# Sparse attention of a two-layer decoder: query norm applied before the split, compressed softmax in two steps

## The chip, the cores and the metric

The kernel runs on one core of one Trainium2 chip. The metric is the time of one execution on the device in microseconds (us), measured beside other runs of the same kernel; the median of three runs of the kernel before is 995.87 us (995.0 to 997.96). Engines are named as in the profile: PE is TensorE, DVE is VectorE, ACT is ScalarE, POOL is GpSimd, SP is SyncE.

## The reference, cut to what matters

The whole program is a decoder trunk of two layers on 256 tokens of width 1024. Each layer has two SwiGLU half-steps around an attention: stick-breaking in the first layer, a sparse attention with three branches in the second. The change lies in the second attention alone:

```python
proj = hn @ w_in
q = proj[..., :NSA_HEADS * Dh].reshape(B, S, NSA_HEADS, Dh)
q = _apply_rope(_rmsnorm(q, q_norm), cos, sin).reshape(B, S, G, R, Dh)
gates = jax.nn.sigmoid(proj[..., NSA_HEADS * Dh:]...)
s_c = jnp.einsum('btgrd,bcgd->bgrtc', q, k_c) * scale
p_c = jax.nn.softmax(jnp.where(valid_c, s_c, NEG), axis=-1) * any_valid
o_c = jnp.einsum('bgrtc,bcgd->btgrd', p_c, v_c)
...
o_s = _nsa_selected(q, sel_idx, k_s, v_s)
o_w = _nsa_window(q, k_w, v_w)
o = gates[0] * o_c + gates[1] * o_s + gates[2] * o_w
return o.reshape(B, S, NSA_HEADS * Dh) @ w_out
```

There are 16 query heads of 64 columns in 4 groups that share keys and values. The root-mean-square norm of a query is one number per token and head. Rotation (rope) and the scores are linear in the query, so that number can be multiplied in anywhere between the projection and the exponential.

## The kernel before, in words

Tokens lie in two tiles of 128 partitions. All arithmetic is to single precision: each operand of a matmul is split into a part that TensorE takes exactly (`hi`, a rounded copy made on ScalarE) and a remainder (`lo`, a subtraction on VectorE), and `mm3` (lines 289 to 292) issues three matmuls for each product. Weights go through the same split: `Weights.pump` (line 201) copies on ScalarE (line 222) and subtracts on VectorE (line 226).

The program is written as one list. A list scheduler orders each engine's instructions by their place in the text and by when their inputs are expected, so that an instruction that is expected late lets others pass; `tc.keep_in_program_order` holds one at its place. On the chip each engine takes its list strictly in order.

The sparse attention is the function `nsa` (line 1332). Its queries come in three projection blocks of two, three and three pairs of heads (`Q_BLOCKS`), each computed in four pieces (`proj_block`, line 587). For a block:

- `q_evac` (line 1348) takes the projection out of PSUM with the weights of the norm (line 1356, VectorE) and its squares (line 1359, ScalarE); block 0 also has the gates.
- `q_turn` (line 1371) rotates on GpSimd (lines 1375 to 1379), splits (ScalarE copy, line 1380; VectorE subtraction, line 1381) and then works out the norm factor `rq`: a sum on VectorE (line 1385), logarithm and exponential on ScalarE (1387, 1388), and four tiny GpSimd operations, one Newton step (1389 to 1392). The factor isn't multiplied into the queries.
- `q_trans` (line 1394) transposes the split queries on TensorE, into banks `aux` (two, taken in turn), and copies them to `qs` (line 1404, ScalarE).

For each of the 16 heads then:

- `scores` (line 1406) issues eight matmuls (line 1417) for masks and scores of both token tiles against own, window and compressed keys; VectorE takes the negated maxima of four pieces (1434, 1435) and multiplies them by the norm factor (1437); ScalarE makes four exponentials with bias and scale from memory (1440 of 128 columns, 1445 of 256), each followed by a read of its accumulated sum, and copies the compressed scores to `cs` (1442); VectorE inverts the sums (1449), GpSimd multiplies in the gate (1450) and scales the probabilities `P` (1453, 256 and 512 columns).
- `ptrans` (line 1480) transposes the probabilities, three transposes for each of two branches (line 1492), and splits them (ScalarE 1494, VectorE 1495); the tiles are named `PT` or, where an old tile is used again, `hT_m`.
- `values` (line 1497) issues six matmuls against the values into `O`; each fourth call adds the compressed branch and splits the output (1515, 1516).

The compressed scores of four heads together go through `cmp_soft` (line 1455): maximum (VectorE 1459), subtraction (GpSimd 1460), product with the norm factor (GpSimd 1461), exponential (ScalarE 1463), sum and inverse (VectorE 1464, 1465), and two GpSimd products with the gate (1466, 1469). `cmp_trans` (line 1471) transposes and splits the result.

The order is written out by hand. While blocks 1 and 2 are projected, the table `plan` (line 1523) says what follows piece i of block b: the transposes of block 0's queries after piece (1, 2), scores of heads 0, 1 and 2 after (1, 3), (2, 0) and (2, 1), the transposes of block 1 and of head 0's probabilities after (2, 2). Then come scores 3, `ptrans(1)`, scores 4, and the loop at line 1560 over n from 1 to 15: a weight split, at n = 1 the whole `q_turn` of block 2, its transposes at n = 3 and n = 6, `cmp_soft` at n = 1, 4, 8 and 12, `cmp_trans` at n = 3, 7, 11 and 15, `ptrans(n + 1)`, `scores(n + 4)`, from n = 12 on a part of the output projection, and `values(n - 1)`.

Of the kernel before, what the change touches and what calls it, by code (L numbers as in the profile page):

```python
# [258 lines left out]
def build(tc, ctx, a, out):  # L259
# [1072 lines left out]
    def nsa(hT, rs, post, targets, st):  # L1332
        kD, V, vcB = st["kD"], st["V"], st["vcB"]
        tc.keep_in_program_order(nc.scalar.preload_act_table_set("natural_log_exp_and_others"))
        with tc.tile_pool(name="ns", bufs=1) as sp:
# [9 lines left out]
            qw, Pm, PT, cs, Ox = {}, {}, {}, {}, {}  # L1345
            heads = [(2 * sc + i, hh) for sc in range(4) for hh in range(2) for i in range(2)]

            def q_evac(b, o):
# [20 lines left out]
                return lambda: q_turn(w, sq, n, h0)  # L1369

            def q_turn(w, sq, n, h0):
                hi, qv = w[:, :, 0:n, 0, :], w[:, :, 0:n, 1, :]
                c, sn = [cst[:, x:x + 32].rearrange("p (t i) -> p t i", t=2).unsqueeze(2) for x in (C_COS, C_SIN)]
# [5 lines left out]
                nc.gpsimd.tensor_tensor(qv[:, :, :, 0:16], t1, t2, op=OP.add)  # L1379
                nc.scalar.activation(hi.bitcast(R), qv, AF.Copy)  # L1380
                nc.vector.tensor_tensor(qv, qv, hi, op=OP.subtract)
                r = rq[:, :, h0:h0 + n]
# [23 lines left out]
            def scores(n, banks=accs):  # L1406
# [26 lines left out]
                r = rq[:, :, 2 * p + hh]  # L1433
# [3 lines left out]
                nc.vector.tensor_tensor(m, m, r.unsqueeze(2).to_broadcast([P, 2, 2]), op=OP.mult)  # L1437
                pr = Pm[n] = sp.tile([P, 768], F32, tag="P", bufs=4, name="P")
                for b in range(2):
                    nc.scalar.activation(pr[:, b * P:(b + 1) * P], va[:, b, :], AF.Exp, bias=nm[:, 0, b:b + 1],  # L1440
                                         scale=r[:, 0:1], accum_out=nm[:, 1, b:b + 1])
                nc.scalar.activation(cs[sc][:, :, 2 * (p % 2) + hh, :], sa[:, 256:288].rearrange("p (t c) -> p t c", t=2),
                                     AF.Copy)
                for b in range(2):
                    nc.scalar.activation(pr[:, 256 + b * 256:512 + b * 256].rearrange("p (k s) -> p k s", k=2),
                                         vb[:, b, :, :], AF.Exp, bias=nm[:, 0, 2 + b:3 + b],
                                         scale=r[:, 1:2], accum_out=nm[:, 1, 2 + b:3 + b])
# [6 lines left out]

            def cmp_soft(sc):

                v = cs[sc].rearrange("p t n i -> p (t n) i")
                mx = sp.tile([P, 2, 8], F32, tag="cm", bufs=2, name="cm")
                nc.vector.tensor_reduce(mx[:, 0, :], v, axis=AX.X, op=OP.max)
                nc.gpsimd.tensor_tensor(v, v, mx[:, 0, :].unsqueeze(2).to_broadcast([P, 8, 16]), op=OP.subtract)  # L1460
                nc.gpsimd.tensor_tensor(cs[sc], cs[sc], rq[:, :, 4 * sc:4 * sc + 4].unsqueeze(3).to_broadcast([P, 2, 4, 16]),
                                        op=OP.mult)
                nc.scalar.activation(v, v, AF.Exp)
                nc.vector.tensor_reduce(mx[:, 0, :], v, axis=AX.X, op=OP.add)
# [53 lines left out]
            def zbanks(name):  # L1518
# [4 lines left out]
            plan = {(1, 2): [lambda: q_trans(0)],  # L1523
                    (1, 3): [lambda: scores(0, zbanks)],
                    (2, 0): [lambda: scores(1)],
                    (2, 1): [lambda: scores(2, zbanks)],
                    (2, 2): [lambda: q_trans(1), lambda: ptrans(0)]}
            for b in range(3):
                o = accs("qp")
                n = Q_COLS[b]  # L1530
                pc = proj_block(n, hT, b == 0, post, [x[:, 0:n] for x in o])
                for i, f in enumerate(pc):
                    f()
                    for g in plan.get((b, i), ()):
                        g()
                turn = q_evac(b, o)
                if b < 2 or not True:
                    turn()
# [21 lines left out]
            for n in range(1, 16):  # L1560
# [4 lines left out]
                if n == 1:  # L1565
                    turn()
                if n == 3:
# [3 lines left out]
                if n == 1 or n % 4 == 0:  # L1571
                    cmp_soft(sc)
# [4 lines left out]
                if n + 4 < 16:  # L1577
                    scores(n + 4)
                if n >= 12:
# [189 lines left out]
```

## Time and profile before

| | us |
|---|---|
| median of 3 runs | 995.87 |
| lowest, highest | 995.0, 997.96 |
| the profiled execution | 994.79 |
| its span (first to last instruction) | 993.0 |

| engine | busy us, whole span | instructions |
|---|---|---|
| PE | 983.4 | 4961 |
| DVE | 873.7 | 1149 |
| ACT | 698.2 | 1099 |
| POOL | 114.9 | 184 |

The sparse attention, from its first projection to its output projection, lies at about 714 to 810 us of the span; its loop over the heads begins at about 745. In rows in order of time, the columns are start, duration, engine, line, operation, output and input, shape and count; the bracket at the end of a row is the idle time of the engine ahead of it and what ended it. In rows of groups, the mean duration in ns stands after the busy time. Instructions of one engine overlap at their ends, so that the distance between two starts can be shorter than the duration of the first.

### The profile page before, as it was taken

To read this page: it belongs to the slowest core of one execution; us is meant where nothing else is said; L and a number is where in the kernel's file an instruction comes from. 1 tells how busy PE (TensorE), PEld (TensorE's weight loads), DVE (VectorE), ACT (ScalarE), POOL (GpSimd) and SP (SyncE) were. 2 spreads that over 40 slices of the span, in tenths; PEclk is the share of its full clock that TensorE was granted. 3 is DMA by queue.
4 is the path that set the end of the run, shared out by engine and by line. 5 is a ranking of instruction groups with operands and counts; after the bars stand their busy time and mean duration, and the time that the engine had idled before them with its cause. 6 is when DMAs were issued, how large, how long until landed. Compare 5 with 4: busy or idle time off the path is not lost.

```text
span 993.0 us, 14093 instructions
## 1 busy us (share of the span) xinstructions
PE 983.4 (99%) x4961; PEld 817.1 (82%) x4961; DVE 873.7 (88%) x1149; ACT 698.2 (70%) x1099; POOL 114.9 (12%) x184
## 2 busy tenths in 40 slices
PE   9999999999999999999999999999999999999998
PEld 6787888898988788878888887888897888788887
DVE  7899999878879999999778698898668879999996
ACT  6776767577868767777565775666669958767763
POOL 0000000010000000000217101000056500000000
PEclk9999999999999999999999999999999999999999
DMA  9988774599846978775996789667330186977761
GB/s 332 355 244 254 222 211 144 176 303 292 247 151 225 332 230 250 235 208 171 273 318 206 252 278 245 235 207 219 114 121 1 45 311 228 310 231 216 250 170 43
DMA packets 65479, 219.89 MB, mean 221 GB/s; under 512 B 7168, under 2 KB 9216, under 8 KB 65408
## 3 DMA queue, kind: packets, MB, share of 16 engines
q1 hardware_dynamic: 58336, 197.86, 58.3%
q0 software_dynamic: 6784, 20.97, 12.1%
q8 instruction: 39, 0.64, 0.3%
q14 instruction: 32, 0.26, 0.1%
q10 hardware_dynamic: 288, 0.16, 0.1%
HBM read 212.67 MB, written 13.63 MB: 228 GB/s over the span
## 4 chain that ended last, share of the span: by engine, by line
PE 69%; issue 13%; DVE 8%; DMA 4%; ACT 3%; POOL 2%; SPq 0%; ACTq 0%; DVEq 0%; POOLq 0%
PE o L291 6%; PE o L292 6%; PE o L290 6%; PE c L290 5%; PE c L292 5%; PE c L291 5%; DVE wl L226 4%; PE a L290 3%; PE a L292 2%; PE a L291 2%; PE cu L290 2%; PE cu L292 2%; PE cu L291 2%; DMA keep<-in_f1i 2%; PE qk L948 2%
## 5 line engine op out<-in xcount | busy, mean ns | idle before, releaser
L226 DVE TENSOR_TENSOR wl<-wraw,wh 128x1024 fp32r<-128x1024 f32 (+2 forms) x316 | 377.1, 1210 | 37.4 <-ACT wh L222 35.7
L222 ACT ACTIVATE wh<-wraw 128x1024 fp32r<-128x1024 f32 (+2 forms) x316 | 322.6, 1044 | 71.1 <-PE o L292 23.8
L222 ACT ACTIVATE wh<-keep 128x1024 fp32r<-128x1024 f32 x112 | 116.6, 1056 | 68.5 <-DVE keep L234 48.8
L226 DVE TENSOR_TENSOR wl<-keep,wh 128x1024 fp32r<-128x1024 f32 x112 | 132.7, 1216 | 6.2 <-ACT wh L222 5.9
L234 DVE TENSOR_TENSOR keep<-keep,wraw 128x1024 f32<-128x1024 f32 x80 | 97.2, 1215 | 1.6 <-DMA wraw<-in_f1i 1.6
L291 PE MATMUL o<-wl,gTh0f 128*128 128x512 f32 x192 | 75.0, 391 | 0.3 <-DVE wl L226 0.3
L290 PE MATMUL o<-wh,gTh0f 128*128 128x512 f32 x192 | 74.8, 397 | 0.0
L292 PE MATMUL o<-wh,gTl0f 128*128 128x512 f32 x192 | 74.6, 391 | 0.0
L290 PE MATMUL o<-wh,gTh1f 128*128 128x512 f32 (+1 forms) x160 | 62.5, 399 | 0.0
L291 PE MATMUL o<-wl,gTh1f 128*128 128x512 f32 (+1 forms) x160 | 62.1, 388 | 0.0
L292 PE MATMUL o<-wh,gTl1f 128*128 128x512 f32 (+1 forms) x160 | 61.3, 388 | 0.0
L290 PE MATMUL a<-wh,hT_f 128*128 128x512 f32 x144 | 57.5, 399 | 0.0
L290 PE MATMUL c<-wh,hT_f 128*128 128x512 f32 x144 | 56.6, 393 | 0.0
L292 PE MATMUL a<-wh,hT_f 128*128 128x512 f32 x144 | 56.3, 391 | 0.0
L291 PE MATMUL a<-wl,hT_f 128*128 128x512 f32 x144 | 56.3, 391 | 0.0
L291 PE MATMUL c<-wl,hT_f 128*128 128x512 f32 x144 | 56.2, 390 | 0.0
L292 PE MATMUL c<-wh,hT_f 128*128 128x512 f32 x144 | 56.2, 390 | 0.0
L290 PE MATMUL cu<-wh,sums 128*128 128x512 f32 x112 | 44.6, 398 | 1.0 <-ACT cp L754 1.0
L290 PE MATMUL c<-wh,sums 128*128 128x512 f32 x112 | 44.3, 396 | 0.1
L292 PE MATMUL cu<-wh,sums 128*128 128x512 f32 x112 | 43.8, 391 | 0.0
L292 PE MATMUL c<-wh,sums 128*128 128x512 f32 x112 | 43.7, 390 | 0.0
L291 PE MATMUL c<-wl,sums 128*128 128x512 f32 x112 | 43.6, 389 | 0.0
(346 smaller groups left out, 2365.0 us busy)
## 6 DMA issues: line engine op xcount, KB each, us to landing
wraw<-in_f1i SPq DMA_DIRECT2D x76, 512.0 KB, 4.8
wraw<-in_f2i SPq DMA_DIRECT2D x68, 512.0 KB, 5.0
wraw<-in_f1o SPq DMA_DIRECT2D x44, 512.0 KB, 4.7
wraw<-in_f2o SPq DMA_DIRECT2D x44, 512.0 KB, 4.8
wraw<-in_sbqk SPq DMA_DIRECT2D x16, 512.0 KB, 4.6
wraw<-sf SPq DMA_DIRECT2D x16, 512.0 KB, 4.5
keep<-in_f2i SPq DMA_DIRECT2D x16, 512.0 KB, 4.5
keep<-in_f2i POOLq DMA_DIRECT2D x16, 512.0 KB, 8.8
```

Source lines behind the costliest of these rows:

```text
L222: i = nc.scalar.activation(hi[:, 0:n], raw[:, 0:n], AF.Copy)
L226: e.tensor_tensor(lo[:, 0:n], raw[:, 0:n], hi[:, 0:n].bitcast(F32), op=OP.subtract)
L234: nc.vector.tensor_tensor(t, y, raw, op=OP.add)
L290: nc.tensor.matmul(o, xh, wh, start=start, stop=False, skip_group_check=True)
L291: nc.tensor.matmul(o, xh, wl, start=False, stop=False, skip_group_check=True)
L292: nc.tensor.matmul(o, xl, wh, start=False, stop=stop, skip_group_check=True)
L948: nc.tensor.matmul(oi, wh[:, c], xh, start=k == 0 and q == 0, stop=False, skip_group_check=True)
```

## The change

Queries are multiplied by their norm factor on GpSimd between rotation and split (`q_scale`). So scores come out normed: the product of the maxima with the factor, the scale operands of the four exponentials, and the product of the compressed scores with the factor go. `q_turn` becomes four steps, rope, norm, scale and split. Blocks 0 and 1 run all four at once; block 2 runs them at n = 1 (rope ahead of the transposes, norm after the scores), n = 2 and n = 3, and its first transposes move from n = 3 to n = 4. The compressed softmax is cut in two: maximum and subtraction (`cmp_max`) at n = 1, 4, 8 and 12, now after the scores, and the rest (`cmp_soft`) at n = 2, 5, 9 and 13, with its exponential and sum held in program order. Everything in `plan` moves one piece later.

```diff
-                return lambda: q_turn(w, sq, n, h0)
+                return q_turn(w, sq, n, h0)
 
             def q_turn(w, sq, n, h0):
                 hi, qv = w[:, :, 0:n, 0, :], w[:, :, 0:n, 1, :]
+                return [lambda: q_rope(qv, n), lambda: q_norm(sq, n, h0), lambda: q_scale(qv, n, h0), lambda: q_split(hi, qv)]
...
+            def q_scale(qv, n, h0):
+                nc.gpsimd.tensor_tensor(qv, qv, rq[:, :, h0:h0 + n].unsqueeze(3).to_broadcast([P, 2, n, DH]), op=OP.mult)
+
+            def q_split(hi, qv):
                 nc.scalar.activation(hi.bitcast(R), qv, AF.Copy)
                 nc.vector.tensor_tensor(qv, qv, hi, op=OP.subtract)
...
-                m = nm[:, 0, :].rearrange("p (t b) -> p t b", t=2)
-                nc.vector.tensor_tensor(m, m, r.unsqueeze(2).to_broadcast([P, 2, 2]), op=OP.mult)
...
                     nc.scalar.activation(pr[:, b * P:(b + 1) * P], va[:, b, :], AF.Exp, bias=nm[:, 0, b:b + 1],
-                                         scale=r[:, 0:1], accum_out=nm[:, 1, b:b + 1])
+                                         accum_out=nm[:, 1, b:b + 1])
...
-                                         scale=r[:, 1:2], accum_out=nm[:, 1, 2 + b:3 + b])
+                                         accum_out=nm[:, 1, 2 + b:3 + b])
...
-            def cmp_soft(sc):
+            def cmp_max(sc):
...
                 nc.gpsimd.tensor_tensor(v, v, mx[:, 0, :].unsqueeze(2).to_broadcast([P, 8, 16]), op=OP.subtract)
-                nc.gpsimd.tensor_tensor(cs[sc], cs[sc], rq[:, :, 4 * sc:4 * sc + 4].unsqueeze(3).to_broadcast([P, 2, 4, 16]),
-                                        op=OP.mult)
-                nc.scalar.activation(v, v, AF.Exp)
-                nc.vector.tensor_reduce(mx[:, 0, :], v, axis=AX.X, op=OP.add)
+
+            def cmp_soft(sc):
...
+                tc.keep_in_program_order(nc.scalar.activation(v, v, AF.Exp))
+                tc.keep_in_program_order(nc.vector.tensor_reduce(mx[:, 0, :], v, axis=AX.X, op=OP.add))
...
-            plan = {(1, 2): [lambda: q_trans(0)],
-                    (1, 3): [lambda: scores(0, zbanks)],
-                    (2, 0): [lambda: scores(1)],
-                    (2, 1): [lambda: scores(2, zbanks)],
-                    (2, 2): [lambda: q_trans(1), lambda: ptrans(0)]}
+            plan = {(1, 3): [lambda: q_trans(0)],
+                    (2, 0): [lambda: scores(0, zbanks)],
+                    (2, 1): [lambda: scores(1)],
+                    (2, 2): [lambda: scores(2, zbanks)],
+                    (2, 3): [lambda: q_trans(1), lambda: ptrans(0)]}
...
                 if n == 1:
-                    turn()
-                if n == 3:
+                    rope()
+                if n == 4:
                     q_trans(2, (5,))
...
-                if n == 1 or n % 4 == 0:
-                    cmp_soft(sc)
...
+                if n == 1:
+                    norm()
+                if n == 2:
+                    scale()
+                if n == 3:
+                    split()
+                if n == 1 or n % 4 == 0:
+                    cmp_max(sc)
+                if n == 2 or n % 4 == 1 and n > 1:
+                    cmp_soft(sc)
```

More of the change, by code (lines that the diff above doesn't have):

```diff
@@ L1344, in nsa @@
                 nc.gpsimd.memset(x[64:128].bitcast(F32), 0.0)
-            qw, Pm, PT, cs, Ox = {}, {}, {}, {}, {}
+            qw, Pm, PT, cs, cm, Ox = {}, {}, {}, {}, {}, {}
             heads = [(2 * sc + i, hh) for sc in range(4) for hh in range(2) for i in range(2)]
@@ L1379, in q_turn, with q_norm @@
                 nc.gpsimd.tensor_tensor(qv[:, :, :, 0:16], t1, t2, op=OP.add)
+            def q_scale(qv, n, h0):
+                nc.gpsimd.tensor_tensor(qv, qv, rq[:, :, h0:h0 + n].unsqueeze(3).to_broadcast([P, 2, n, DH]), op=OP.mult)
+            def q_split(hi, qv):
                 nc.scalar.activation(hi.bitcast(R), qv, AF.Copy)
                 nc.vector.tensor_tensor(qv, qv, hi, op=OP.subtract)
+            def q_norm(sq, n, h0):
                 r = rq[:, :, h0:h0 + n]
@@ L1453, in scores @@
                     nc.gpsimd.tensor_tensor(x, x, nm[:, 2, j:j + 2].unsqueeze(2).to_broadcast([P, 2, w]), op=OP.mult)
+            def cmp_max(sc):
+                v = cs[sc].rearrange("p t n i -> p (t n) i")
+                mx = cm[sc] = sp.tile([P, 2, 8], F32, tag="cm", bufs=2, name="cm")
+                nc.vector.tensor_reduce(mx[:, 0, :], v, axis=AX.X, op=OP.max)
+                nc.gpsimd.tensor_tensor(v, v, mx[:, 0, :].unsqueeze(2).to_broadcast([P, 8, 16]), op=OP.subtract)
             def cmp_soft(sc):
                 v = cs[sc].rearrange("p t n i -> p (t n) i")
[L1458 to L1461, printed above, removed]
-                                        op=OP.mult)
-                nc.scalar.activation(v, v, AF.Exp)
-                nc.vector.tensor_reduce(mx[:, 0, :], v, axis=AX.X, op=OP.add)
+                mx = cm[sc]
+                tc.keep_in_program_order(nc.scalar.activation(v, v, AF.Exp))
+                tc.keep_in_program_order(nc.vector.tensor_reduce(mx[:, 0, :], v, axis=AX.X, op=OP.add))
                 nc.vector.reciprocal(mx[:, 0, :], mx[:, 0, :])
@@ L1536, in nsa @@
                 turn = q_evac(b, o)
-                if b < 2 or not True:
-                    turn()
+                while b < 2 and turn:
+                    turn.pop(0)()
+            rope, norm, scale, split = turn
             oo = None
@@ L1565, in nsa @@
                 if n == 1:
-                    turn()
-                if n == 3:
+                    rope()
+                if n == 4:
                     q_trans(2, (5,))
```

2 lines of the change are left out of this document (1 added, 1 removed).

## The prediction

> **What bounds the kernel now.** I read the page's span and busy rows first, then the busy time by stage over the sparse attention, then ScalarE's and TensorE's rows in order of time there, and last the groups of that stretch.
>
> ```profile
> span 993.0 us, 14093 instructions
> PE 983.4 (99%) x4961; PEld 817.1 (82%) x4961; DVE 873.7 (88%) x1149; ACT 698.2 (70%) x1099; POOL 114.9 (12%) x184
> ```
>
> Over the whole program TensorE is the engine that is never free, and 70% for ScalarE (ACT) looks harmless. The stages say otherwise. The columns are span, then busy time and count for PE, PEld, DVE, ACT and POOL, then the granted clock, the DMA share and GB/s:
>
> ```profile
> 715.00:727.24 12.24, 12.24 (x78) 11.85 (x77) 10.87 (x19) 8.49 (x16) 4.54 (x8) 1.00 0.73 232
> 727.24:744.77 17.53, 17.44 (x114) 15.44 (x114) 10.48 (x25) 12.41 (x40) 9.81 (x21) 1.00 0.16 58
> 744.77:787.24 42.47, 40.30 (x271) 33.70 (x270) 34.44 (x90) 41.25 (x155) 26.48 (x52) 1.00 0.01 1
> 787.24:798.00 10.76, 10.76 (x58) 8.84 (x57) 10.14 (x17) 9.90 (x16) 4.15 (x7) 1.00 0.53 179
> ```
>
> From 744.77 to 787.24, the loop over the heads, ScalarE works 41.25 of 42.47 us; nowhere else in the attention is it that full. PE shows 40.30, but its matmul ends are modelled, so I price its work by starts. One head's three parts follow, each met once with nothing waiting: the scores from 763.37 to 764.49, the values from 764.49 to 765.62 with the eight query transposes behind them to 766.49, six probability transposes from 772.08 to 772.73. The first and the last row bound the eleven heads that I count.
>
> ```profile
> 743.52 0.29 PE L1417 MATMUL S<-mns,identb 128*128 128x288 bf16 x1
> 763.37 0.30 PE L1417 MATMUL S<-mns,identb 128*128 128x288 bf16 x1
> 764.49 0.48 PE L290 MATMUL O<-PT,Vh 128*128 128x512 f32 x1
> 765.62 1.04 PE L1402 MATMUL qTp<-cst,qw 128*128 128x128 f32 x8
> 766.49 0.29 PE L1417 MATMUL S<-mns,identb 128*128 128x288 bf16 x1
> 772.08 0.82 PE L1492 MATMUL pt<-cst,P 128*128 128x128 f32 x6
> 772.73 0.27 PE L1417 MATMUL S<-mns,identb 128*128 128x256 bf16 x1
> 781.01 0.30 PE L1417 MATMUL S<-mns,identb 128*128 128x288 bf16 x1
> ```
>
> So a score group is 1.12 us of PE, a head's values 1.13, its transposes 0.65. Between 743.52 and 781.01 stand eleven score groups (12.3), ten heads' values (11.3) and transposes (6.5), twelve query transposes at 0.87 for eight (1.3), and about 1.8 for the twelve compressed-value matmuls and four small transposes (an estimate: half a values matmul each): 33.2 of 37.49 us. PE therefore has 4.3 us of stops in the loop. That is the most the loop can give before PE itself is the limit, however fast the others get. These rows are where the stops are plainest; the bracket names the wait and what ended it, and in the second row three transposes take 0.88 instead of half of 0.82:
>
> ```profile
> 746.63 0.28 PE L1417 MATMUL S<-mns,identb 128*128 128x288 bf16 x1 [0.34 <-ACT cs L1442]
> 749.66 0.88 PE L1492 MATMUL pt<-cst,P 128*128 128x128 f32 x3
> 752.14 0.50 PE L290 MATMUL O<-hT_m,Vh 128*128 128x512 f32 x1 [0.90 <-ACT hT_m L1494]
> 768.75 0.49 PE L290 MATMUL O<-hT_m,Vh 128*128 128x512 f32 x1 [0.25 <-ACT hT_m L1494]
> 769.62 0.38 PE L1475 MATMUL ct<-cst,cs 128*64 128x128 f32 x2 [0.38 <-DVE hT_m L1495]
> ```
>
> Three of the four named waits end with ScalarE, the fourth with a VectorE copy that stands behind ScalarE's. ScalarE paces the loop, TensorE is close behind.
>
> **The exponentials lose their scale operand.** Each of the 16 heads has four, with a bias and a scale read from memory per partition. In the loop ScalarE's starts follow each other without gaps, so the step from one start to the next is its price:
>
> ```profile
> 744.77 0.84 ACT L1380 ACTIVATE qw<-qw 128x768 fp32r<-128x768 f32 x1 [0.50 <-POOL qw L1379]
> 745.52 0.44 ACT L1440 ACTIVATE P<-S,nm,rq 128x128 f32<-128x128 f32 x1
> 745.86 0.19 ACT L1440 ACTIVATION_READ_ACCUMULATOR P<-S,nm,rq 128x1 f32 x1
> ...
> 746.47 0.57 ACT L1445 ACTIVATE P<-S,nm,rq 128x256 f32<-128x256 f32 x1
> 746.92 0.21 ACT L1445 ACTIVATION_READ_ACCUMULATOR P<-S,nm,rq 128x1 f32 x1
> ...
> 750.92 0.31 ACT L1463 ACTIVATE cs<-cs 128x128 f32<-128x128 f32 x1 [0.70 <-POOL cs L1461]
> ...
> 751.24 0.85 ACT L1494 ACTIVATE hT_m<-pt 128x384 fp32r<-128x384 f32 x2
> 751.98 0.46 ACT L1440 ACTIVATE P<-S,nm,rq 128x128 f32<-128x128 f32 x1
> ```
>
> An exponential of 128 columns steps 0.34, one of 256 steps 0.45; one of 384 would step 0.56. A plain copy of 384, without operands, steps 0.37 (two in 0.74). Two operands are thus worth 0.19, one 0.09. The one-operand copy against the plain one says the same, 475 against 379 ns:
>
> ```profile
> L1135 ACT ACTIVATE kva<-kv,rstd 128x256 f32<-128x256 f32 x4 | 1.9, 475 | 3.6 <-PE kv L292 3.6
> L620 ACT ACTIVATE rBqk<-rB 128x256 f32<-128x256 f32 x1 | 0.4, 379 | 0.0
> L1445 ACT ACTIVATE P<-S,nm,rq 128x256 f32<-128x256 f32 x26 | 15.0, 609 | 0.0
> L1453 POOL TENSOR_TENSOR P<-P,nm 128x512 f32<-128x512 f32 x12 | 12.5, 1043 | 0.0
> L1453 POOL TENSOR_TENSOR P<-P,nm 128x256 f32<-128x256 f32 x12 | 7.4, 615 | 0.9
> L1437 DVE TENSOR_TENSOR nm<-nm,rq 128x4 f32<-128x4 f32 x12 | 2.5, 204 | 0.2
> L1461 POOL TENSOR_TENSOR cs<-cs,rq 128x128 f32<-128x128 f32 x3 | 1.2, 404 | 0.2
> ```
>
> No exponential with a bias alone is in this trace: the saving lies between 0 (both reads overlap) and 0.19, and I take 0.09, the one-operand row. The loop has 26 pairs (x26 at L1445 and as many at L1440), so 52 x 0.09 = 4.7 us of ScalarE's 42.47 go; the other twelve exponentials lie beside the projection and pay nothing.
>
> **What else leaves the loop.** The product of maximum and norm (L1437, 204 ns a head on VectorE) goes, ahead of the exponentials. On POOL the product of compressed scores and norm goes (404 ns). ScalarE stood 0.70 us at 750.92 behind that, inside the third block's norm; with the maximum taken one head and the exponential the next, POOL has a head's time, and I take that wait as gone. The third block's split, 0.75 of step at 744.77 ahead of the first head's exponentials, moves to n = 3. It is still paid, where ScalarE then has room.
>
> **What is added.** Three products on POOL, in place. L1453 gives 1.04 us for 512 columns and 0.62 for 256, so 1.04 for the first block and, by the same slope, 1.47 for the others. In the loop that is 1.47 less three times 0.40, on an engine busy 26.48 of 42.47: nothing on the path, since the third block's queries are needed at n = 4 and the product is issued at n = 2. If POOL's cover went, it would cost its 1.47. The matmuls stay as they are.
>
> **What is moved.** Query transposes and the first three score groups come one projection piece later. PE's work is the same, but behind the last piece nothing of the projection is left to fill waits: query transposes of block 1, head 0's transposes, scores 3, head 1's transposes, scores 4. ScalarE must empty the two banks these transposes alternate in, which before had projection matmuls beside it. And block 0 has a longer way to its transposes: norm, product, split. Before:
>
> ```profile
> 724.07 1.86 POOL L1389 TENSOR_TENSOR qn<-qn 128x8 f32<-128x8 f32 x1 [2.55 <-ACT qn L1388]
> ...
> 726.59 0.20 POOL L1392 TENSOR_TENSOR rq<-qn 128x8 f32<-128x8 f32 x1
> 723.18 2.69 DVE L226 TENSOR_TENSOR wl<-wraw,wh 128x768 fp32r<-128x768 f32 x3
> 722.22 0.69 DVE L1381 TENSOR_TENSOR qw<-qw 128x512 f32<-128x512 f32 x1 [0.46 <-ACT qw L1380]
> 721.55 0.63 ACT L1380 ACTIVATE qw<-qw 128x512 fp32r<-128x512 f32 x1 [1.49 <-POOL qw L1379]
> 727.24 0.30 PE L1417 MATMUL S<-mns,identb 128*128 128x288 bf16 x1
> ```
>
> PE reached head 0's scores at 727.24, right behind piece four of block 1; without the 0.87 of query transposes ahead it gets there at 726.4 and now wants the transposes. If the norm is ready at 726.8 as before, product (1.04), split (0.63) and subtraction (0.69) end at 729.2, 2.8 us late. The norm no longer waits for the subtraction of 722.22, though, and three short POOL products need not take until 726.8; and projection matmuls can go first where the list order lets them. Between 0 and 2.8 us I take 0.5, near the lower end, because PE still has block 2's projection to put ahead.
>
> **The sum.** Of 4.3 us of PE stops I keep 1.2: waits for the compressed transposes, the third block's split (0.75) in its new place, and the limit that PE and ScalarE, now at 36.5 (42.47 less 4.7 and its 1.22 idle) against 38.2, share (38.2 is 42.47 less 4.3). The loop gives 3.1; the start costs 0.5. The profiled execution took 994.79 us (span 993.0 and 1.8 around it), so 994.79 - 2.6 = 992.2; the median of the three runs, 995.87, is 1.08 above that execution, and I forecast 993.3. Behind 787.24 PE is busy 10.76 of 10.76, so nothing more is won there and, as the weight loads follow the loop, nothing is lost. About 0.3% (3.0 us) is what a measurement of this kernel can tell from no change.
>
> **Rivals.** *All stops go.* ScalarE's 36.5 us leave it 1.7 below PE's 38.2, so PE could run through: 994.79 - 4.3 + 1.08 = 991.6. Against it speak the 0.38 us behind a VectorE copy, which no operand touches.
>
> *POOL is held up under block 0.* The 1.86 us at 724.07 for eight columns, against 0.20 for the same size at 726.59, ends where VectorE's three subtractions (723.18 to 725.87) end. A product of 512 columns that meets such a stretch ends up to 2.7 late, and PE, which takes its list in order, stops for the whole 2.8 instead of 0.5: 995.6. [...]
>
> *Slower: ScalarE waits on POOL at the compressed exponentials.* These are now held in program order, so ScalarE cannot pass them. If the subtraction ahead of each stands behind one head's pair of products on POOL (0.62 + 1.04 = 1.66), all four wait that long: 6.6 us on the engine that paces the loop, 993.3 + 6.6 = 999.9. It decides from the point where these waits exceed the 2.6 us won, 0.65 each. For it speaks the 0.70 at 750.92; against it, that POOL now has a head of about 3.4 us (37.49 / 11).
>
> *The operand costs nothing beside another.* Then ScalarE keeps its 4.7 us and only the 0.70 wait goes, about 1.0 with what follows it, less 0.5: 994.79 - 0.5 + 1.08 = 995.4.
>
> **How the numbers follow.** Forecast 0.48, all stops 0.17, POOL held up 0.15, ScalarE behind POOL 0.11, operand free 0.09. Faster by over 0.3% means below 992.9: all of the second and somewhat under half of the forecast's own spread (991.9 to 994.9, from 0 to 2.2 of stops kept), 0.39. Slower by over 0.3%, above 998.9: most of the fourth and the far tail of the third, 0.12. The rest, 0.49, is within 0.3%. The range goes from 990.7 (all stops gone, taken from the lowest of the three runs, 995.0) to 997.0 (POOL held up, and 1.4 us more of the loop's stops kept), and leaves out the slow case.
>
> **What would show it.** Exponentials of 256 columns near 0.36 from start to start, and ScalarE's idle time in the loop up by some us; heads at PE near 3.1 us from score group to score group instead of 3.4; no wait above 0.5 us on ScalarE ahead of the compressed exponentials; PE's stop ahead of the first query transposes below 1 us. I am wrong if the exponentials keep 0.45, if the stop at block 0 passes 2 us, or if the loop keeps 37.5 us for eleven heads.

## The result, and the profile after

The changed kernel takes 1005.98 us (median of 4 runs, 1004.11 to 1006.87) beside 995.89 us (995.0 to 997.96) of the kernel before on the same chip: ratio 1.0095, 95% interval 1.0082 to 1.0108. It is slower by about 10 us. A later measurement of the same kernel gave 1005.97 us, ratio 1.0097 (1.0084 to 1.0110). In three of the experiments below one execution took far longer than the others (1079.98, 3162.38 and 3365.43 us): their times are the medians of the other executions, and the trace of the first, which is of that execution, is not read.

The page of the profiled execution (1006.35 us, 1.8 of it around the span), span and busy time:

```profile
span 1004.5 us, 14068 instructions
PE 985.1 (98%) x4961; PEld 818.2 (81%) x4961; DVE 871.2 (87%) x1133; ACT 693.1 (69%) x1099; POOL 118.9 (12%) x183
```

ScalarE works 5.1 us less than before, VectorE 2.5 less, GpSimd 4.0 more, TensorE 1.7 more with the same 4961 matmuls. ScalarE and VectorE have less to do, and the time grew. The operand did what was forecast; these are ScalarE's rows of one head in order of time:

```profile
756.29 0.36 ACT L1447 ACTIVATE P<-S,nm 128x128 f32<-128x128 f32 x1
756.54 0.21 ACT L1447 ACTIVATION_READ_ACCUMULATOR P<-S,nm 128x1 f32 x1
...
757.05 0.49 ACT L1452 ACTIVATE P<-S,nm 128x256 f32<-128x256 f32 x1
757.41 0.23 ACT L1452 ACTIVATION_READ_ACCUMULATOR P<-S,nm 128x1 f32 x1
```

From start to start an exponential of 128 columns takes 0.25 (before 0.34), one of 256 takes 0.36 (before 0.45): 0.09 each. What was lost stands in the view of TensorE's waits from 700 to 1000 us; the columns are tile and line that waited, what ended the wait, and us in total, times, longest; these are its first five rows:

```profile
PE ct L1485 <- POOL cs L1479: 5.4, 3, 2.6
PE c L290 <- ACT cp L754: 1.4, 1, 1.4
PE qTp L1412 <- issue: 1.1, 1, 1.1
PE hTp L535 <- DVE h L529: 0.7, 1, 0.7
PE qTp L1412 <- DVE qw L1389: 0.6, 1, 0.6
```

Before, TensorE waited for none of these (its list there has 0.38 at a ct, behind a copy and not behind GpSimd). Where they cost is seen when TensorE's matmuls are counted in both traces and the start of the same number compared (from the attention on the order differs in places, so that equal numbers mean about equal amounts of work there, not the same instruction; `f21` is the program's last SwiGLU half-step):

| matmul no. | before | after | difference | between the rows lies |
|---|---|---|---|---|
| 3000 | 594.90 | 596.07 | 1.17 | the start of the program, outside the change |
| 3640 | 727.63 | 730.14 | 2.51 | the first query transposes |
| 3720 | 740.64 | 743.58 | 2.94 | the projection's end |
| 3800 | 754.37 | 755.60 | 1.23 | the first heads of the loop: 1.7 won |
| 3840 | 760.34 | 765.29 | 4.95 | first compressed transposes: 3.7 lost |
| 3880 | 766.17 | 770.69 | 4.52 | |
| 4000 | 784.62 | 792.81 | 8.18 | third compressed transposes: 3.7 lost |
| 4160 | 814.93 | 824.13 | 9.20 | |
| 4840 | 965.61 | 976.92 | 11.30 | 160 us, to the end of `f21`: 2.1 lost, 1.6 of it at one stop in `f21` |

(The differences are taken before rounding.) The 1.7 won and the first 3.7 lost are uncertain by some half a microsecond, since just there the two orders differ.

The first place is the product ahead of the query transposes. In order of time, GpSimd, ScalarE, VectorE, TensorE:

```profile
724.04 0.90 POOL L1400 TENSOR_TENSOR qn<-qn 128x8 f32<-128x8 f32 x1
725.03 0.78 POOL L1401 TENSOR_SCALAR qn<-qn 128x8 f32<-128x8 f32 x1
726.18 1.04 POOL L1385 TENSOR_TENSOR qw<-qw,rq 128x512 f32<-128x512 f32 x1
727.26 0.63 ACT L1388 ACTIVATE qw<-qw 128x512 fp32r<-128x512 f32 x1 [2.83 <-POOL qw L1385]
727.92 0.69 DVE L1389 TENSOR_TENSOR qw<-qw 128x512 f32<-128x512 f32 x1 [2.17 <-ACT qw L1388]
728.71 1.06 PE L1412 MATMUL qTp<-cst,qw 128*128 128x128 f32 x8 [1.10 <-issue]
```

Norm, product, split and subtraction follow each other with nothing between them, and TensorE stands 1.10 us at their end. The second is the compressed softmax of the first four heads: subtraction, exponential, then GpSimd's queue up to the last product, and the transposes:

```profile
753.36 0.40 POOL L1467 TENSOR_TENSOR cs<-cs,cm 128x128 f32<-128x128 f32 x1
755.54 0.46 ACT L1473 ACTIVATE cs<-cs 128x128 f32<-128x128 f32 x1
755.57 0.21 POOL L1399 TENSOR_TENSOR qn<-qn 128x12 f32<-128x12 f32 x1
...
756.74 1.48 POOL L1385 TENSOR_TENSOR qw<-qw,rq 128x768 f32<-128x768 f32 x1
...
758.45 1.61 POOL L1460 TENSOR_TENSOR P<-P,nm 128x256 f32<-128x256 f32 x2
...
760.30 0.40 POOL L1479 TENSOR_TENSOR cs<-cs,cm 128x128 f32<-128x128 f32 x1
760.76 0.41 PE L1485 MATMUL ct<-cst,cs 128*64 128x128 f32 x2 [2.63 <-POOL cs L1479]
```

ScalarE does not wait ahead of its exponential, it only comes to it 1.8 us after the subtraction's end. The products behind it then stand in GpSimd's queue behind the third block's norm and scale (755.57 to 758.2) and a head's probabilities. Before, the same chain was done ahead of its transposes:

```profile
750.00 0.40 POOL L1460 TENSOR_TENSOR cs<-cs,cm 128x128 f32<-128x128 f32 x1
753.98 0.41 POOL L1469 TENSOR_TENSOR cs<-cs,cm 128x128 f32<-128x128 f32 x1
755.42 0.38 PE L1475 MATMUL ct<-cst,cs 128*64 128x128 f32 x2
```

The third softmax has no query block ahead of it. Its products were slow instead; GpSimd, VectorE, TensorE:

```profile
785.79 2.55 POOL L1460 TENSOR_TENSOR P<-P,nm 128x256 f32<-128x256 f32 x2
788.58 1.43 POOL L1479 TENSOR_TENSOR cs<-cs,cm 128x128 f32<-128x128 f32 x1
785.65 1.22 DVE L226 TENSOR_TENSOR wl<-wraw,wh 128x1024 fp32r<-128x1024 f32 x1
788.54 1.21 DVE L226 TENSOR_TENSOR wl<-wraw,wh 128x1024 fp32r<-128x1024 f32 x1
790.07 0.59 PE L1485 MATMUL ct<-cst,cs 128*64 128x128 f32 x2 [2.33 <-POOL cs L1479]
```

2.55 instead of 1.61 and 1.43 instead of 0.40, each beside a subtraction of VectorE's weight split (L226) that starts with it. These splits come with the output projection, which begins at n = 12. The stop is followed by a second loss, in the view by stretches (the column behind POOL is the granted clock):

```profile
790.00:793.00 3.00, 2.93 (x10) 2.52 (x11) 1.26 (x3) 1.98 (x10) 1.78 (x4) 0.53 0.60 175
```

TensorE ran at 0.53 for three microseconds behind the 2.33 us stop, so at least 1.4 us more of the 3.7 are the clock.

### The profile page after: what moved, and what is told of

The parts are those of the page before. It is cut to its first block, busy times and chain, and to the rows that moved or that the text cites. A ratio compares the mean times of both kernels' runs of the same rounds, so it can differ in the third digit from the quotient of the medians.

```text
span 1004.5 us, 14068 instructions
## 1 busy us (share of the span) xinstructions
PE 985.1 (98%) x4961; PEld 818.2 (81%) x4961; DVE 871.2 (87%) x1133; ACT 693.1 (69%) x1099; POOL 118.9 (12%) x183
## 4 chain that ended last, share of the span: by engine, by line
PE 72%; issue 11%; DVE 5%; ACT 4%; DMA 4%; POOL 3%; SPq 0%; POOLq 0%; ACTq 0%; DVEq 0%
PE o L292 7%; PE o L291 7%; PE o L290 7%; PE c L290 6%; PE c L292 6%; PE c L291 6%; PE a L290 3%; PE a L291 3%; PE a L292 3%; PE cu L290 3%; PE cu L291 2%; PE cu L292 2%; DVE wl L226 2%; PE qk L948 2%; PE gTp L666 1%
## 5 line engine op out<-in xcount | busy, mean ns | idle before, releaser
L226 DVE TENSOR_TENSOR wl<-wraw,wh 128x1024 fp32r<-128x1024 f32 (+2 forms) x316 | 377.1, 1209 | 40.8 <-ACT wh L222 38.8
L226 DVE TENSOR_TENSOR wl<-keep,wh 128x1024 fp32r<-128x1024 f32 x112 | 132.8, 1217 | 8.3 <-ACT wh L222 7.9
```

What stands on the lines that cost most here:

```text
L226: e.tensor_tensor(lo[:, 0:n], raw[:, 0:n], hi[:, 0:n].bitcast(F32), op=OP.subtract)
```

## The experiments

Two theories. **A**: the loss is TensorE waiting at places whose input GpSimd now delivers later: the compressed softmax, spread over two heads and queued behind the third block, and the scale product ahead of the first query transposes. **B**: the loss is not in these waits but in the longer way of the queries itself, the later plan, or the order of instructions, which the list scheduler makes anew after any edit.

**The compressed softmax as before, the rest of the change kept.** Maximum and softmax together at n = 1, 4, 8, 12, ahead of the transposes, not held in order:

```diff
-                if n == 2 or n % 4 == 1 and n > 1:
-                    cmp_soft(sc)
+                if n == 1 or n % 4 == 0:
+                    cmp_max(sc)
+                    cmp_soft(sc)
...
```

> The changed kernel with its compressed softmax in one piece again, at the place it had before (n = 1, 4, 8, 12, ahead of the compressed transposes) and with nothing held in program order; queries are still multiplied on GpSimd, exponentials have no scale operand, the plan is one piece later. Theory A (the loss is the late compressed softmax: TensorE stops at the compressed transposes for 2.63, 0.40 and 2.33 us and then runs 3.41 us at half clock, 1.7 us lost): these 7 us and what follows them go, 996 to 999 us. Theory B (the loss is the queries' way: norm and product on GpSimd, score groups one piece later): 1003 us or more.

1002.64 us, ratio 1.0068 (1.0050 to 1.0087), 0.4 under what theory B said. Only about 3 us came back where theory A, as first put, wanted 7 or more. Where the rest lies in this order is not known, since no trace of it can be read.

**The kernel before, with nothing but the compressed softmax cut in two.** The product by the norm stays, in `cmp_max`:

```diff
-                if n == 1 or n % 4 == 0:
-                    cmp_soft(sc)
...
                     scores(n + 4)
+                if n == 1 or n % 4 == 0:
+                    cmp_max(sc)
+                if n == 2 or n % 4 == 1 and n > 1:
+                    cmp_soft(sc)
```

> The kernel before with nothing but the compressed softmax cut in two, at the places and with the two instructions held in program order as in the changed kernel; its product with the norm factor stays in the first half. Theory A: slower by itself, 999 to 1003 us, with TensorE waiting at the compressed transposes, though the first of them (n = 3) may wait less, since the third block's norm and product are not in GpSimd's queue ahead of it. Theory B: no change, 995 to 997 us.

1000.12 us, ratio 1.0045 (1.0029 to 1.0061), as theory A had it: without any other part of the change, but with the new order that the scheduler makes of it, it costs 4.4 us. TensorE's rows; the second wait ends with VectorE and not with GpSimd:

```profile
760.51 0.41 PE L1480 MATMUL ct<-cst,cs 128*64 128x128 f32 x2 [1.40 <-POOL cs L1474]
787.54 0.41 PE L1480 MATMUL ct<-cst,cs 128*64 128x128 f32 x2 [1.24 <-DVE nm L1437]
```

The two stops are 2.6 of the 4.4 us. Behind the first the granted clock was 0.51 from 761.5 to 764.9, which makes 1.7 more.

**The change without the two lines that hold the exponential and the sum in order.**

```diff
-                tc.keep_in_program_order(nc.scalar.activation(v, v, AF.Exp))
-                tc.keep_in_program_order(nc.vector.tensor_reduce(mx[:, 0, :], v, axis=AX.X, op=OP.add))
+                nc.scalar.activation(v, v, AF.Exp)
+                nc.vector.tensor_reduce(mx[:, 0, :], v, axis=AX.X, op=OP.add)
```

> The changed kernel without the two instructions held in program order (exponential and sum of the compressed softmax); all else as changed. If holding them is what makes the compressed softmax late (the second one's exponential starts 9.5 us after its input is ready, at 770.59 against 761.06), most of the 7 us go: 997 to 1000 us. If the place in the text alone does it, the exponential still comes late: 1004 to 1007 us.

1003.43 us, ratio 1.0071 (1.0050 to 1.0091), between the two forecasts. The third stop at ct is gone, the first is still there, with the clock at 0.52 behind it (763.0 to 766.5), and in `f21` TensorE stops 2.28 instead of 1.40. So holding the two in order makes the third stop and not the first:

```profile
761.74 0.41 PE L1485 MATMUL ct<-cst,cs 128*64 128x128 f32 x2 [2.62 <-POOL cs L1479]
```

**The kernel before without the operands, twice.** First by the source:

```diff
-                nc.vector.tensor_tensor(m, m, r.unsqueeze(2).to_broadcast([P, 2, 2]), op=OP.mult)
+                nc.vector.tensor_tensor(m, m, one[:, :, 0:1].to_broadcast([P, 2, 2]), op=OP.mult)
...
-                                         scale=r[:, 0:1], accum_out=nm[:, 1, b:b + 1])
+                                         accum_out=nm[:, 1, b:b + 1])
...
```

> The kernel before with the scale operands of the four exponentials left out and the product of the maxima made with ones, so that the norm is left out of the own and window exponentials; instructions and their order are meant to stay. This measures the operand by itself. If one operand costs 0.09 us from start to start and ScalarE paces the loop, 4.7 us of ScalarE go and the time falls by 1.5 to 3 us, to 993 to 994.5. If ScalarE does not pace the loop, 995.5 to 996.3, with the exponentials' step at 0.36 all the same. If the operand costs nothing, the step stays 0.45.

1000.46 us, ratio 1.0050 (1.0032 to 1.0067): slower, a miss for both forecasts of the time. The instructions were the same but for one that writes the ones, their order was not: given shorter exponentials, the scheduler moved some two hundred of them, and new stops appeared:

```profile
755.85 0.41 PE L1477 MATMUL ct<-cst,cs 128*64 128x128 f32 x2 [1.46 <-POOL cs L1471]
813.73 0.66 PE L535 MATMUL hTp<-cst,h 128*128 128x128 f32 x4 [1.95 <-DVE h L529]
```

So the operand was exchanged again, this time after scheduling, with every instruction left at its place:

```diff
...
+    for block in fn.blocks:
+        for k, i in enumerate(list(block.instructions)):
+            if "Activation" in type(i).__name__ and len(i.ins) == 4 and getattr(i.ins[2], "memref", "").startswith("rq_"):
...
+                block.instructions[k] = copy.replace(i, ins=[i.ins[0], i.ins[1], one, i.ins[3]])
```

> The kernel before with every instruction at its old place on every engine: once the order is settled, the scale operand of the 64 exponentials is exchanged for the constant 1, and the last Newton product writes 1 into rq (so the norm of the queries is left out of the result). Theory A (the operand's 0.09 us on 52 exponentials lies on ScalarE's path in the head loop, and the loss of the changed kernel comes from order alone): the exponentials of 256 columns start 0.36 apart instead of 0.45, the loop shrinks by 2 to 3 us, 992.5 to 994.5. Rival (the stops of the loop belong to other waits and the operand is beside the path): steps of 0.36 too, but 995.3 to 996.3. That the operand-free exponentials themselves cost time, as the unpinned trial without operands could be read (1000.9): 999 and above.

995.34 us, ratio 0.9992 (0.9982 to 1.0001). The median is 0.6 us under that of the kernel before (995.97), not told apart from it; matmul by matmul its trace gains 1.0 us on that of before between number 3708 and 4104, the attention from its last projection piece to 803 us. The exponentials step 0.36, as both theories said, and the time is the rival's. The stretch of eleven score groups, first of before and then of this run, with three rows of ScalarE and TensorE from it in order of time:

```profile
743.52:781.01 37.49, 35.32 (x238) 29.13 (x235) 30.34 (x83) 35.77 (x134) 24.12 (x50) 1.00 0.00 1
```

```profile
743.28:780.24 36.96, 34.98 (x238) 29.05 (x235) 30.07 (x83) 32.79 (x135) 24.10 (x50) 1.00 0.00 1
750.65 0.31 ACT L1463 ACTIVATE cs<-cs 128x128 f32<-128x128 f32 x1 [1.39 <-POOL cs L1461]
750.96 0.85 ACT L1494 ACTIVATE hT_m<-pt 128x384 fp32r<-128x384 f32 x2
751.87 0.49 PE L290 MATMUL O<-hT_m,Vh 128*128 128x512 f32 x1 [0.91 <-ACT hT_m L1494]
```

ScalarE (fourth busy time) lost 2.98 us of work, the stretch 0.53. The largest stop, 0.90 before, is still 0.91. It ends with ScalarE's copy `hT_m`, but it isn't ScalarE's load that makes it: the copy stands in ScalarE's queue behind the compressed exponential (L1463), and this waits for GpSimd's product. ScalarE waited there for 0.70 us before and for 1.39 now, so that the time it had saved ahead of this row went into a longer wait.

**The later plan alone, and the scaling alone.** The kernel before with the new `plan`; then the change with plan, third block and compressed softmax as before, so that scaling and missing operands are what is left.

> The kernel before with only the plan of the projection moved one piece later (first query transposes at piece 3 of block 1 and so on); operands, maxima, compressed softmax and third block as before. Theory A (the plan costs only what the first heads start later, since the projection's pieces fill TensorE meanwhile): no stop ahead of the first query transposes, one score group fewer under the projection, 996 to 998. Rival B (the later plan is what costs: TensorE runs the loop with one head's lead less): 1000 to 1003. A gain (the 0.9 to 1.3 us waits at the first transposes go): 994 to 995.5.

995.75 us, ratio 0.9994 (0.9985 to 1.0003): the plan costs nothing.

> The changed kernel with the plan, the third block and the compressed softmax as they were before: what is left of the change is the scaling on GpSimd ahead of the split and the exponentials without operand. Theory A: TensorE stands up to 3 us at the first query transposes, since their queries pass through the longer GpSimd chain a piece earlier, against some 2 us won in the loop: 996 to 999. Rival B (the scaling on GpSimd is itself the loss: its products and the reordering that goes with it hold up the heads): 1001 to 1004. A gain that the other parts spoil: 993 to 995.5.

1005.27 us, ratio 1.0093 (1.0075 to 1.0112), over what theory A (996 to 999) and rival B (1001 to 1004) said. Its rows show the scale product as the plan's other half: without the later plan TensorE stands 2.14 us at the first transposes and makes them at half the clock (0.50 granted from 728 to 731; 1.94 for eight instead of 1.06), and the heads behind start late. Two more stops, 1.65 at 796.55 and 2.25 in `f21`, lie far behind the queries:

```profile
728.12 1.94 PE L1412 MATMUL qTp<-cst,qw 128*128 128x128 f32 x8 [2.14 <-issue]
744.24 0.66 PE L1412 MATMUL qTp<-cst,qw 128*128 128x128 f32 x4 [1.28 <-ACT qs L1414]
759.29 0.50 PE L1427 MATMUL S<-kDh,qs 128*128 128x512 f32 x1 [2.25 <-ACT P L1452]
```

So the parts don't add up: the softmax alone costs 4.4 us, the scaling alone 9.3, the whole change 10.1. Each has an order of its own.

**The change with the compressed transposes one head later, with the third block behind the softmax, and with both.** Each leaves all other parts in place:

```diff
-                if n % 4 == 3:
-                    cmp_trans(sc)
+                if n % 4 == 0:
+                    cmp_trans(sc - 1)
```

with `cmp_trans(3)` ahead of `values(15)`; and for the third block, its first transposes moved from n = 4 to n = 5:

```diff
-                if n == 1:
-                    norm()
-                if n == 2:
-                    scale()
-                if n == 3:
-                    split()
...
                     cmp_soft(sc)
+                if n == 2:
+                    norm()
+                if n == 3:
+                    scale()
+                if n == 4:
+                    split()
```

> The changed kernel with the compressed transposes one head later. Theory A (TensorE stands at them behind the last product on GpSimd, 2.63 and 2.33 us, and then runs at half clock): no wait over 0.5 us ahead of a ct transpose, the half clock at 790 gone, 999 to 1001.5; what is left over 995.9 is the late first query transposes (1.3) and the order of the copies behind. Rival (the loss is spread over the order and the queries' path, and TensorE only waits elsewhere for the same engines): 1003 to 1006.

999.04 us, ratio 1.0032 (1.0022 to 1.0042): 6.9 us come back, the sum as theory A had it. Its mechanism held for one of two stops: the third fell to 0.17, the first stayed, now with a half clock of its own (0.50 from 761 to 764). Counted as in the table, 3.6 us lie at the third softmax, none at the first, and 1.2 at the stop in `f21`, which fell from 1.40 to 0.5; that the sum came out is in part luck:

```profile
760.83 0.63 PE L1485 MATMUL ct<-cst,cs 128*64 128x128 f32 x2 [2.84 <-POOL cs L1479]
788.31 0.41 PE L1485 MATMUL ct<-cst,cs 128*64 128x128 f32 x2 [0.17 <-POOL cs L1479]
```

> The changed kernel with the third block's norm, scale and split one head later each, behind the first compressed softmax, and its first query transposes one head later. Theory A (the last compressed product comes late because the norm and the 1.48 us scale stand ahead of it in GpSimd's queue, 2.6 us in all): the first ct stop (2.63 us) falls under 0.5 us, the one of the third softmax with its half clock stays, 1001.5 to 1003.5. Rival (it is late because the softmax itself is issued two heads after its scores, whatever GpSimd does meanwhile): the first stop stays over 1.5 us, 1005 to 1007.

1001.69 us, ratio 1.0061 (1.0048 to 1.0074), in theory A's range. With the third block out of the way the first stop falls from 2.63 to 0.96 (more was expected), so GpSimd's queue is what made most of it. The third, which was to stay, fell too, from 2.33 to 1.13, and the clock behind it stayed at 1.00: by the table's count 2.4 us of the gain lie there, so the time fits for another reason than the one given:

```profile
758.96 0.41 PE L1485 MATMUL ct<-cst,cs 128*64 128x128 f32 x2 [0.96 <-POOL cs L1479]
787.03 0.41 PE L1485 MATMUL ct<-cst,cs 128*64 128x128 f32 x2 [1.13 <-POOL cs L1479]
```

> Both remedies: third block behind the first compressed softmax, and every compressed transpose one head later. Theory A (all that the compressed softmax costs is TensorE's wait for its last product): no ct wait over 0.5 us, 995 to 997.5, what is left being the 1.1 us ahead of the first query transposes against 1 us won by the operand. Rival (a share of the loss is the reordering that any edit brings): 998.5 to 1001 with no ct wait.

997.61 us, ratio 1.0018 (1.0008 to 1.0027), just above theory A's range and below its rival's, with one ct wait of 1.23 left. Run again beside the unchanged change on one chip:

> The run with both remedies once more, for a second profile of it beside the same neighbours. Theory A1: 997 to 998.3 with the stop of over 1 us ahead of c in f21 again. Theory A2: 997 to 998.3, and in a profile near the median the stop is under 0.6 us.

> The changed kernel itself once more, unchanged, as the neighbour of the run with the pinned copy: 1005 to 1006.5. Theory A1: the stop in f21 is 1.2 to 1.8 us again in its profile; theory A2: it comes out otherwise by over 0.5 us.

998.26 us (ratio 1.0021, 1.0013 to 1.0030) against 1005.97: the two moves give back 7.7 us.

**A plan later still.** Both moves, and:

```diff
-            plan = {(1, 3): [lambda: q_trans(0)],
-                    (2, 0): [lambda: scores(0, zbanks)],
-                    (2, 1): [lambda: scores(1)],
-                    (2, 2): [lambda: scores(2, zbanks)],
-                    (2, 3): [lambda: q_trans(1), lambda: ptrans(0)]}
+            plan = {(2, 0): [lambda: q_trans(0)],
+                    (2, 1): [lambda: scores(0, zbanks)],
+                    (2, 2): [lambda: scores(1)],
+                    (2, 3): [lambda: scores(2, zbanks), lambda: q_trans(1), lambda: ptrans(0)]}
```

> The same with the plan a second piece later, so that the first query transposes stand behind one more piece of the projection. Theory A (the 1.1 us stop there goes, and the lost lead costs nothing, as in the trial of the plan alone): 994 to 996.5, at least 0.5 under the run with both remedies. Rival (with two pieces less lead the heads start without the scores ahead, TensorE waits for ScalarE at the loop's start): 997 to 1000.

1003.02 us, ratio 1.0073 (1.0060 to 1.0087): the rival, and worse than it said. The stop at the first transposes is gone, but the second block's transposes wait 2.52 us and a ct stop of 2.7 us is back, each with about half the clock behind it (0.57 and 0.58 over 4 us). One piece of lead was free in the kernel before; two are not free here.

```profile
747.22 0.66 PE L1412 MATMUL qTp<-cst,qw 128*128 128x128 f32 x4 [2.52 <-ACT qs L1414]
```

**The stop in `f21`.** In the profile of the change ScalarE stands 1.74 us at a weight split whose DMA is late, and the copy `cp` that TensorE wants is behind it: the last product that `cp` reads stands at 965.02 for 0.39 us, but the copy starts at 967.54, behind the split of 966.58. Before, the copy stood one place earlier and started at 955.91, right behind its product (955.49 for 0.39 us).

```profile
966.58 1.06 ACT L222 ACTIVATE wh<-keep 128x1024 fp32r<-128x1024 f32 x1 [1.74 <-DMA keep<-in_f2i]
967.54 0.58 ACT L754 ACTIVATE cp<-c 128x512 f32<-128x512 f32 x1
968.17 0.50 PE L290 MATMUL c<-wh,sums 128*128 128x512 f32 x1 [1.40 <-ACT cp L754]
```

For the last gate pair of `f21` (`W.pin` set there) the copy is emitted ahead of the last split and held in order with the splits; the rest of the order stays but for a row or two on TensorE:

```diff
                         W.done()
+                        if copied and u == 1:
+                            copied()
                         W.pump()
...
-                    nc.scalar.activation(x, o, AF.Copy)
+                    i = nc.scalar.activation(x, o, AF.Copy)
+                    if W.pin:
+                        tc.keep_in_program_order(i)
```

Tried on the run with both moves and on the change:

> The run with both remedies, and in the last gate pair of f21 ScalarE's copy cp stands one place earlier, ahead of the split that waits for its DMA; on the other engines the order stays but for one swap of TensorE's rows. Theory A (the 1.75 us stop ahead of c at 961.89 comes from that one place in ScalarE's queue): the stop goes, 1.5 to 1.8 us less than the run with both remedies, 995.5 to 996.5. Rival (TensorE only waits there for the same DMA by another way): the stop moves on to the next product, 997 to 998.

997.65 us, ratio 1.0018 (1.0008 to 1.0028). The stop was 1.75 in the profile of the first run with both moves, is gone here, and the median is what it was. In the second profile of the same unpinned program it is not there either, and that execution took 997.57 us where the first had taken 999.94, the highest of its eleven.

> The changed kernel with nothing but ScalarE's copy cp of the last gate pair one place earlier (on TensorE one row of the same stretch moves with it). Theory A1 (the 1.40 us stop at 968.17 is part of the loss in every execution): 1.2 to 1.8 us less than the changed kernel beside it on the same chip. Theory A2 (the stop is there only when that DMA comes late, as in the execution that was profiled, or what stands behind takes it up; so the run with both remedies and the one with the pinned copy had one median): within 0.5 us of it.

1004.39 us, ratio 1.0082 (1.0065 to 1.0098), beside 1005.97 (1.0084 to 1.0110). 1.6 us less, as A1 has it, and the unpinned change had the stop in both its profiles (1.40 and 1.42); but the intervals overlap, and the clock is a rival: the mean granted clock of single executions goes from 0.996 to 0.998 in both programs, and those at 0.998 took the least time (1001.74 and 1002.67 pinned, 1004.67 unpinned). With both moves the stop shows in one of two profiles (A2). For the change itself it is likely, not settled.

**Both moves and the pinned copy, without the scale product of block 0.**

```diff
+                if b == 0:
+                    del turn[2]
                 while b < 2 and turn:
                     turn.pop(0)()
```

> The same without the scale product of block 0 on GpSimd (the first four heads' pairs are left unscaled, so their result is left out), the order of the other engines kept but for one place on ScalarE. Theory A (the 1.1 us stop ahead of the first query transposes is this product, 1.04 us, and nothing else is left of the loss): the stop falls under 0.2 us, about 1 us less than the run with the pinned copy, 994.5 to 995.5, under the kernel before by the 0.9 us that the operand was worth at a fixed order. Rival (the stop is set by the norm's own products, slowed to 0.9 and 0.8 us, or by the split behind): the stop stays over 0.6 us, 995.5 to 996.5.

995.63 us, ratio 0.9994 (0.9985 to 1.0002), 2.0 us less than the same with the product (expected 1), and not told apart from the kernel before. With the product the stop had been 1.39 in its profile; now TensorE reaches the transposes without one, as theory A said, while the time lies just over its range:

```profile
727.41 1.03 PE L1422 MATMUL qTp<-cst,qw 128*128 128x128 f32 x8
```

**The account.** On the medians: 1005.97 to 998.26 by moving the compressed transposes and the third block (7.7), 997.65 to 995.63 by the one product (2.0); 998.26 and 997.65 come from two measurements and differ by the pinned copy. The rest is within 0.4 us of the kernel before. The traces of 1005.97 and 998.26 differ by 7.0 us, counted as in the table: 4.8 of them by number 4100, at the compressed transposes and their clock, 0.6 up to `f21`, and 1.6 in `f21`, which no theory had. So theory A holds for its places, for somewhat less than the moves gave back. Theory B's later plan, by itself, is refuted (995.75). Its reordering is real: it turned the operand-free kernel into a slower one, and no experiment here parts it from the stops, which come and go with the order.

## Why the prediction was wrong

**ScalarE paces the loop: this failed.** It was read from 41.25 busy of 42.47. At a fixed order ScalarE lost 2.98 us and the loop 0.53. "PE has 4.3 us of stops" came from a count of 33.2 us of work; the profile's own busy time of that stretch is 35.32, so 2.2 of stops was the better reading, and the largest, 0.90, was untouched by the operand. It hung on GpSimd: ScalarE stood at the compressed exponential, and the copy that TensorE wanted stood behind it. The term "the loop gives 3.1" measures 0.5 to 1.0 for the operand alone; in the change the eleven heads lost 2.25 (39.74 against 37.49).

**0.09 us an operand: right**, 0.34 to 0.25 and 0.45 to 0.36. So were the 1.04 and 1.47 us of the products (1.04, 1.48).

**"With the maximum taken one head and the exponential the next, POOL has a head's time": the step that failed most.** ScalarE's wait did go, and with it the 0.90 stop. But the transposes kept their place at n = 3, and what was given to the subtraction was taken from the products behind the exponential. Before, the last product started at 753.98 and its transposes at 755.42; after, the product was done at 760.70, and the transposes had been due at 758.13. I asked whether the first wait goes, not when the last consumer is due.

**"Nothing on the path, since the third block's queries are needed at n = 4": failed.** Nearly true of the queries (their transposes waited 0.56 us for the split at 763.78), but the products stand in one queue with the compressed softmax. With them behind it the first stop fell from 2.63 to 0.96.

**The late first transposes**, 0.5 taken from 0 to 2.8: the stop was 1.10, and taking the product away gave 2.0. The rival named for it (POOL held up by VectorE's subtractions) did not reach the product, which took its 1.04; only the norm ahead of it was held up, 0.90 and 0.78 for eight columns that usually take 0.20, as it had been before (1.86). The place was right and the size too small.

**"Behind 787.24 nothing is lost": failed.** The third compressed transposes fall there, under VectorE's weight splits, with the half clock (0.53 behind the 2.33 us stop).

**The slower rival** had the place (compressed exponentials held in order, GpSimd behind) and the sign, at 999.9 us, but its mechanism did not occur: no row of L1473 has a wait ahead of it. TensorE waited at the end of the chain instead, which the prediction's test "no wait above 0.5 us on ScalarE ahead of the compressed exponentials" could not see. Of its three conditions for being wrong one was met: eleven heads take 39.74 us (with the probability transposes of one head more than the 37.49 before, 0.65).

```profile
745.60:785.34 39.74, 35.61 (x244) 29.78 (x241) 29.37 (x71) 33.90 (x136) 23.69 (x45) 1.00 0.01 1
```

## What to carry to other kernels

When a chain is spread over more steps, look at when its last consumer is due and at everything queued ahead of its last step on that engine; a wait that goes at the head of the chain may come back at its end. An engine that is 97% busy in a stretch is not shown to pace it: look whether the other engines' waits end with its load or with a wait of its own. To price one operand or instruction in a kernel laid out by a list scheduler, change it after scheduling, because an edit to the source may reorder the rows behind it, some two hundred here.

## What the runs showed of the hardware

The granted clock halved behind stops of 2.33 us (the change, 790 us), 2.84 us (transposes one head later) and 2.14 us (scaling alone), and behind one of 1.40 us with another of 0.54 just ahead of it (the softmax cut in two alone), but not behind the 2.63 us stop of the change at 758.13 to 760.76. In the second profile of the same, unchanged program it was the other way round: half behind the first stop (2.62 us, to 760.50), full behind the third (2.33 us, to 790.41). The stretches, first of the run with the later transposes behind its 2.84 us stop, then of the change behind its 2.63 us stop, last of the second profile of the change behind both:

```profile
761.00:764.00 3.00, 3.00 (x14) 2.77 (x14) 0.59 (x2) 2.16 (x11) 2.13 (x4) 0.50 0.00 0
```

```profile
761.00:762.00 1.00, 1.00 (x9) 0.88 (x7) 0.39 (x1) 0.80 (x2) 0.92 (x4) 1.00 0.00 0
```

```profile
762.00:764.00 2.00, 2.00 (x12) 2.00 (x11) 1.88 (x2) 1.16 (x7) 0.65 (x1) 0.50 0.00 0
790.40:793.40 3.00, 2.99 (x16) 2.50 (x17) 1.26 (x3) 2.54 (x12) 2.12 (x4) 1.00 0.55 175
```

So the same stop of the same program can cost its length alone (the third in the second profile of the change, 2.33 us with the clock at 1.00 behind it), or its length and over a microsecond more (the same stop in the first profile, 2.33 us and then 3.00 us at 0.53, which makes 1.4). The length alone doesn't decide: 2.14 us were enough in one run, and 2.63 us were not in another. What else decides is not shown by these runs.

GpSimd products were stretched from 0.40 to 1.43 us (788.58 in the trace of the change) and from 0.20 to 0.90 us (724.04) while VectorE's weight split subtractions ran (788.54 for 1.21 us, and two from 723.93 for 1.82 us together).
